# Mixture of softmaxes: giving each partition 32 adjacent rows instead of every 128th row

## The chip, the cores and the metric

The kernel runs on one core of a Trainium2 chip; the other cores are idle. The metric is the device time of one execution in microseconds (us). Before the change it is 783.3 us (783.3 to 783.43). "The profile" is a hardware trace of one execution; its span is some 2 us shorter than the timed run.

## The reference

```python
batch, seq, vocab, num_heads = 32, 128, 4096, 4
prior_probs = softmax(prior, axis=-1)       # prior  [32, 128, 4]
s = softmax(logits, axis=-1)                # logits [32, 128, 4, 4096], float32
mixture = sum(prior_probs[..., None] * s, axis=2)   # [32, 128, 4096]
```

Numpy's `exp`, maximum and sum are written here as `softmax`. There are 4096 rows (batch times seq). A row is four heads of 4096 floats, so 64 KB to read and 16 KB to write: 268.4 MB in and 67.1 MB out in all.

## The kernel before

A unit of work is one batch element: 128 rows, one to a partition. The load of a unit is one DMA of 8.39 MB (four DMAs of one head each for the first and the last three units), the store one DMA of 2.10 MB. ScalarE (ACT) does the exponentials with their sums, VectorE (DVE) scales and adds the heads, GpSimd (POOL) multiplies two columns for a coefficient. SyncE (SP) issues the loads, ACT most of the stores. Two load tiles alternate.

```python
def pieces(b):
    return 1 if b == 0 or b >= B - 3 else H
def load(b, eng=nc.sync):
    lt = lpool.tile([P, H, V], FP32, name="ltile")        # bufs=2
    n = pieces(b)
    for h in range(0, H, n):
        eng.dma_start(out=lt[:, h : h + n], in_=logits[b, :, h : h + n, :])
def store(b, lo=0, hi=V, eng=nc.sync):
    eng.dma_start(out=out[b, :, lo:hi], in_=accs[b][:, lo:hi])
# ... prior: softmax on [32, 128, 4], then four 32x32 transposes to pp [128, H, 32] ...
for b in range(B):
    # ... store(b - 1, eng=nc.scalar)
    for h in range(H):
        ex = nc.scalar.activation(et, lt[:, h], AF.Exp, accum_out=dsum[:, col])
        nc.vector.reciprocal(rden[:, col], dsum[:, col])
        # h == 0: acc = et * rden * pp;  else coeff = rden * pp; acc += et * coeff
    if b + 2 < B:
        load(b + 2)
```

The softmax here doesn't subtract the row's maximum and nothing guards it: scores larger than these inputs give would overflow.

## Time and profile before

| | before |
|---|---|
| time | 783.3 us |
| DVE busy, ACT busy | 68%, 60% of the span |
| DMA engines busy | 99.7% (two data queues) |
| moved | 335.67 MB at a mean 430 GB/s |

From the profile page of the kernel before, the DMA rows in 40 slices of the span, the packets, and the queues (packets, MB, share of 16 engines):

```profile
DMA  9999999999999999999999999999999999999998
GB/s 373 448 416 440 434 416 456 410 463 405 460 409 456 416 443 429 419 454 415 458 408 450 419 464 406 456 427 430 432 430 439 426 446 412 457 408 430 429 429 364
DMA packets 11143, 335.67 MB, mean 430 GB/s; under 512 B 1248, under 2 KB 1248, under 8 KB 1280
q1 hardware_dynamic: 7056, 276.83, 82.1%
q10 hardware_dynamic: 4080, 58.79, 17.6%
```

A 9 is 90% busy or more. The 16 DMA engines have no idle slice, so they bound the kernel. The table by stretches of the kernel before (start and end, length, busy time of DVE, ACT and POOL, granted clock, DMA share, GB/s) gives the rates:

```profile
0.00:20.00 20.00, 9.98 (x13) 10.60 (x7) 0.40 (x5) 1.00 0.93 377
200.00:400.00 200.00, 136.30 (x69) 120.65 (x66) 4.97 (x26) 1.00 1.00 433
400.00:600.00 200.00, 134.74 (x65) 116.94 (x64) 4.60 (x24) 1.00 1.00 434
760.00:782.00 22.00, 10.93 (x6) 3.71 (x2) 0.38 (x2) 1.00 0.84 359
```

From the waits (engine, line, what it waited for: us in total, times, longest) and from the instructions in order of time (start, length; the first exponential of unit 1, of unit 2 and of unit 28; units count from 0):

```profile
ACT ebuf L107 <- DMA ltile<-in_logits_dram: 241.0, 32, 18.0
45.37 3.62 ACT L107 ACTIVATE ebuf<-ltile 128x4096 f32<-128x4096 f32 x1 [18.04 <-DMA ltile<-in_logits_dram]
67.81 3.62 ACT L107 ACTIVATE ebuf<-ltile 128x4096 f32<-128x4096 f32 x1 [6.40 <-DMA ltile<-in_logits_dram]
696.72 3.62 ACT L107 ACTIVATE ebuf<-ltile 128x4096 f32<-128x4096 f32 x1 [8.14 <-DMA ltile<-in_logits_dram]
```

ACT waits for loads. From unit 2 to unit 28 there are 26 units, of (696.72 - 67.81) / 26 = 24.19 us each; a unit moves 10.49 MB.

### The profile page before, as it was taken

What the parts mean: (1) busy time and instruction counts of PE and PEld (TensorE: products, weight loads), DVE (VectorE), ACT (ScalarE), POOL (GpSimd) and SP (SyncE); (2) the same over time, 40 slices, a digit from 0 to 9 for tenths busy, and PEclk for the clock granted to TensorE, in tenths of its full rate; (3) what the DMA queues carried; (4) which work ended last, traced back from release to release, by engine and by line L of the source; (5) the groups of instructions that cost most, each with busy time, mean ns of one, the idle gap of its engine ahead of it and who ended that gap; (6) DMA issues with size and microseconds to landing.
All of it is one profiled execution on the core that took longest, in us unless ns stands there. A gap on an engine that the chain in (4) does not pass through costs nothing.

```text
span 781.3 us, 851 instructions
## 1 busy us (share of the span) xinstructions
DVE 527.9 (68%) x266; ACT 470.0 (60%) x258; POOL 18.6 (2%) x100
## 2 busy tenths in 40 slices
DVE  4647677666786666865668666677666776668994
ACT  5366556755567555575555765547655577558971
POOL 0000000000000000000000000000000000000000
DMA  9999999999999999999999999999999999999998
GB/s 373 448 416 440 434 416 456 410 463 405 460 409 456 416 443 429 419 454 415 458 408 450 419 464 406 456 427 430 432 430 439 426 446 412 457 408 430 429 429 364
DMA packets 11143, 335.67 MB, mean 430 GB/s; under 512 B 1248, under 2 KB 1248, under 8 KB 1280
## 3 DMA queue, kind: packets, MB, share of 16 engines
q1 hardware_dynamic: 7056, 276.83, 82.1%
q10 hardware_dynamic: 4080, 58.79, 17.6%
q14 instruction: 7, 0.06, 0.0%
HBM read 268.50 MB, written 67.11 MB: 430 GB/s over the span
## 4 chain that ended last, share of the span: by engine, by line
DMA 66%; ACT 14%; DVE 10%; issue 7%; SPq 0%; POOL 0%; DVEq 0%; POOLq 0%; ACTq 0%
DMA ltile<-in_logits_dram 66%; ACT ebuf L107 14%; DVE acc L128 9%; DVE ltile L128 1%; SPq L43 0%; POOL coeff L123 0%; DVE rden L116 0%; DVEq L166 0%; DVE ltile L118 0%; POOLq L166 0%; ACTq L107 0%
## 5 line engine op out<-in xcount | busy, mean ns | idle before, releaser
L107 ACT ACTIVATE ebuf<-ltile 128x4096 f32<-128x4096 f32 x120 | 433.0, 3609 | 284.5 <-DMA ltile<-in_logits_dram 241.0
L128 DVE SCALAR_TENSOR_TENSOR acc<-ebuf,coeff,acc 128x4096 f32<-128x4096 f32 x90 | 403.6, 4484 | 27.4 <-POOL coeff L123 27.4
L116 DVE RECIPROCAL rden<-dsum 128x1 f32<-128x1 f32 x128 | 20.4, 160 | 206.3 <-ACT ebuf L107 206.3
L118 DVE TENSOR_SCALAR acc<-ebuf,rden,pp 128x4096 f32<-128x4096 f32 x30 | 72.4, 2412 | 1.3 <-DVE rden L116 0.3
L123 POOL TENSOR_TENSOR coeff<-rden,pp 128x1 f32<-128x1 f32 x96 | 18.4, 191 | 748.1 <-DVE rden L116 748.1
L107 ACT ACTIVATE ltile<-ltile 128x4096 f32<-128x4096 f32 x8 | 28.9, 3608 | 4.3 <-DMA ltile<-in_logits_dram 4.3
L128 DVE SCALAR_TENSOR_TENSOR ltile<-ltile,coeff 128x4096 f32<-128x4096 f32 (+1 forms) x7 | 27.0, 3874 | 1.8 <-POOL coeff L123 1.8
L107 ACT ACTIVATION_READ_ACCUMULATOR ebuf<-ltile 128x1 f32 x120 | 22.4, 187 | 0.0
L118 DVE TENSOR_SCALAR ltile<-ltile,rden,pp 128x4096 f32<-128x4096 f32 x2 | 4.8, 2412 | 0.1
L58 DVE TENSOR_REDUCE pmax<-pr 32x128 f32<-32x512 f32 x1 | 0.7, 674 | 5.8 <-DMA pr<-in_prior_dram 5.8
L62 ACT ACTIVATE pe<-pc 32x512 f32<-32x512 f32 x1 | 0.6, 628 | 4.8 <-DVE pc L60 4.8
L62 ACT ACT_TABLE_LOAD x1 | 1.3, 1283 | 1.2 <-PEq L155 1.2
L107 ACT ACTIVATION_READ_ACCUMULATOR ltile<-ltile 128x1 f32 x8 | 1.5, 186 | 0.0
L75 DVE STREAM_TRANSPOSE pp<-pn 32x128 f32<-32x128 f32 x4 | 1.2, 302 | 0.1
L64 DVE TENSOR_REDUCE psum<-pe 32x128 f32<-32x512 f32 x1 | 0.7, 674 | 0.7 <-ACT pe L62 0.7
L69 DVE TENSOR_TENSOR pn<-pe,prec 32x512 f32<-32x512 f32 x1 | 1.0, 1042 | 0.0
L66 DVE RECIPROCAL prec<-psum 32x128 f32<-32x128 f32 x1 | 0.9, 941 | 0.0
L60 DVE TENSOR_TENSOR pc<-pr,pmax 32x512 f32<-32x512 f32 x1 | 0.7, 680 | 0.0
L155 POOL MEMSET const-float32-0.0<- 128x1 f32 x1 | 0.1, 99 | 0.2 <-issue 0.2
L155 POOL MEMSET const-bfloat16-1.0<- 128x1 bf16 x1 | 0.1, 102 | 0.0
L155 POOL MEMSET const-uint8-127<- 128x1 uint8 x1 | 0.1, 102 | 0.0
L155 POOL MEMSET const-float32-1.0<- 128x1 f32 x1 | 0.1, 99 | 0.0
## 6 DMA issues: line engine op xcount, KB each, us to landing
out_dram<-acc ACTq DMA_DIRECT2D x28, 2048.0 KB, 29.3
ltile<-in_logits_dram SPq DMA_DIRECT2D x16, 2048.0 KB, 20.5
out_dram<-acc SPq DMA_DIRECT2D x2, 2048.0 KB, 32.9
out_dram<-ltile SPq DMA_DIRECT2D x1, 2048.0 KB, 21.2
out_dram<-ltile SPq DMA_DIRECT2D x2, 1024.0 KB, 8.7
ltile<-in_logits_dram SPq DMA_DIRECT2D x28, 32.3
pr<-in_prior_dram ACTq DMA_DIRECT2D x1, 64.0 KB, 5.0
```

The source lines that it names most:

```text
L58: nc.vector.reduce_max(pmax, pr, axis=AX.X)
L60: nc.vector.tensor_sub(pc, pr, pmax.unsqueeze(2).to_broadcast([B, S, H]))
L62: nc.scalar.activation(pe, pc, AF.Exp)
L64: nc.vector.reduce_sum(psum, pe, axis=AX.X)
L66: nc.vector.reciprocal(prec, psum)
L69: nc.vector.tensor_mul(pn.rearrange("b h s -> b s h"), pe, prec.unsqueeze(2).to_broadcast([B, S, H]))
L75: nc.vector.transpose(pp[32 * t : 32 * (t + 1)], pn[:, :, 32 * t : 32 * (t + 1)])
L107: ex = nc.scalar.activation(et, lt[:, h], AF.Exp, accum_out=dsum[:, col])
L116: nc.vector.reciprocal(rden[:, col], dsum[:, col])
L118: nc.vector.tensor_scalar(out=acc, in0=et, scalar1=rden[:, col], scalar2=pp[:, h, b : b + 1], op0=ALU.mult, op1=ALU.mult,)
L123: nc.gpsimd.tensor_mul(coeff[:, col], rden[:, col], pp[:, h, b : b + 1])
L128: nc.vector.scalar_tensor_tensor(out=acc[:, cs], in0=et[:, cs], scalar=coeff[:, col], in1=acc[:, cs], op0=ALU.mult, op1=ALU.add,)
```

## The change

Each partition gets 32 adjacent rows of the whole input, and unit u is row u of every partition. Then `prior` arrives in the layout in which it is used, and its softmax needs no transposes and fewer tiles. Loads, stores and compute keep their number, shape and order. What else moves is where one DMA reads and writes: neighbouring partitions were 64 KB apart in `logits` and 16 KB in `out`, and are now 2 MB and 512 KB apart (the pitch). "Near" is used below for the old addresses, "wide" for the new ones.

```diff
+    U = B * S // P
+    lg = logits.rearrange("b s h v -> (b s) h v").rearrange("(p u) h v -> u p h v", u=U)
+    ov = out.rearrange("b s v -> (b s) v").rearrange("(p u) v -> u p v", u=U)
+    pv = prior.rearrange("b s h -> (b s) h").rearrange("(p u) h -> p u h", u=U)
...
-            eng.dma_start(out=lt[:, h : h + n], in_=logits[b, :, h : h + n, :])
+            eng.dma_start(out=lt[:, h : h + n], in_=lg[b, :, h : h + n, :])
...
-        eng.dma_start(out=out[b, :, lo:hi], in_=accs[b][:, lo:hi])
+        eng.dma_start(out=ov[b, :, lo:hi], in_=accs[b][:, lo:hi])
...
-    pr = cpool.tile([B, S, H], FP32, name="pr")        # and pc, pe, psum, prec, pn, 4 transposes
-    nc.scalar.dma_start(out=pr, in_=prior)
+    pr = cpool.tile([P, U, H], FP32, name="pr")        # sub, exp, sum, reciprocal in place
+    nc.scalar.dma_start(out=pr, in_=pv)
```

More of the change, by code (lines that the diff above doesn't have):

```diff
@@ L34, in pieces @@
     def pieces(b):
-        return 1 if b == 0 or b >= B - 3 else H
+        return 1 if b == 0 or b >= U - 3 else H
     ltiles = {}
@@ L48, in store @@
     def store(b, lo=0, hi=V, eng=nc.sync):
-        eng.dma_start(out=out[b, :, lo:hi], in_=accs[b][:, lo:hi])
+        eng.dma_start(out=ov[b, :, lo:hi], in_=accs[b][:, lo:hi])
     load(0, eng=nc.sync)
-    pr = cpool.tile([B, S, H], FP32, name="pr")
-    nc.scalar.dma_start(out=pr, in_=prior)
+    pr = cpool.tile([P, U, H], FP32, name="pr")
+    nc.scalar.dma_start(out=pr, in_=pv)
     load(1, eng=nc.sync)
-    pmax = cpool.tile([B, S], FP32, name="pmax")
+    pmax = cpool.tile([P, U], FP32, name="pmax")
     nc.vector.reduce_max(pmax, pr, axis=AX.X)
-    pc = cpool.tile([B, S, H], FP32, name="pc")
-    nc.vector.tensor_sub(pc, pr, pmax.unsqueeze(2).to_broadcast([B, S, H]))
-    pe = cpool.tile([B, S, H], FP32, name="pe")
-    nc.scalar.activation(pe, pc, AF.Exp)
-    psum = cpool.tile([B, S], FP32, name="psum")
-    nc.vector.reduce_sum(psum, pe, axis=AX.X)
-    prec = cpool.tile([B, S], FP32, name="prec")
-    nc.vector.reciprocal(prec, psum)
-    pn = cpool.tile([B, H, S], FP32, name="pn")
-    nc.vector.tensor_mul(
-        pn.rearrange("b h s -> b s h"), pe, prec.unsqueeze(2).to_broadcast([B, S, H])
-    )
-    pp = cpool.tile([P, H, B], FP32, name="pp")
-    for t in range(S // 32):
-        nc.vector.transpose(
-            pp[32 * t : 32 * (t + 1)], pn[:, :, 32 * t : 32 * (t + 1)]
-        )
+    nc.vector.tensor_sub(pr, pr, pmax.unsqueeze(2).to_broadcast([P, U, H]))
+    nc.scalar.activation(pr, pr, AF.Exp)
+    nc.vector.reduce_sum(pmax, pr, axis=AX.X)
+    nc.vector.reciprocal(pmax, pmax)
+    pp = cpool.tile([P, U, H], FP32, name="pp")
+    nc.vector.tensor_mul(pp, pr, pmax.unsqueeze(2).to_broadcast([P, U, H]))
     NCHUNK = 2
-    dsum = cpool.tile([P, B * H], FP32, name="dsum")
-    rden = cpool.tile([P, B * H], FP32, name="rden")
-    coeff = cpool.tile([P, B * H], FP32, name="coeff")
+    dsum = cpool.tile([P, U * H], FP32, name="dsum")
+    rden = cpool.tile([P, U * H], FP32, name="rden")
+    coeff = cpool.tile([P, U * H], FP32, name="coeff")
     ebuf = cpool.tile([P, 2, V], FP32, name="ebuf")
     exps = []
-    for b in range(B):
-        last = b == B - 1
-        inplace = b >= B - 2
+    for b in range(U):
+        last = b == U - 1
+        inplace = b >= U - 2
         lt = ltiles.pop(b)
@@ L99 @@
         acc = accs[b]
-        if 0 < b < B - 3:
+        if 0 < b < U - 3:
             store(b - 1, eng=nc.scalar)
@@ L118 @@
                 nc.vector.tensor_scalar(
-                    out=acc, in0=et, scalar1=rden[:, col], scalar2=pp[:, h, b : b + 1],
+                    out=acc, in0=et, scalar1=rden[:, col], scalar2=pp[:, b, h : h + 1],
                     op0=ALU.mult, op1=ALU.mult,
@@ L122 @@
                 continue
-            nc.gpsimd.tensor_mul(coeff[:, col], rden[:, col], pp[:, h, b : b + 1])
+            nc.gpsimd.tensor_mul(coeff[:, col], rden[:, col], pp[:, b, h : h + 1])
             n = NCHUNK if split else 1
@@ L133 @@
                     store(b, c * w, (c + 1) * w)
-        if b + 2 < B:
+        if b + 2 < U:
             load(b + 2)
-        if b == B - 3:
+        if b == U - 3:
             store(b - 1)
             store(b)
-        elif b == B - 2:
+        elif b == U - 2:
             store(b)
```

## The prediction

> **What bounds the kernel now.** The 16 DMA engines. The page's DMA row reads 9 (90% or more) in 39 of 40 slices and its two data queues take 82.1% and 17.6% of the engines' time, 99.7% together. They move 335.67 MB at a mean 430 GB/s; the table by stretches shows 433 to 434 GB/s from 100 to 600 us, and less only in the first 20 us (377) and the last 22 (359). DVE is busy 68%, ACT 60%. In the waits, ACT waited 241.0 us for loads of ltile. A unit (8.39 MB in, 2.10 MB out) costs 24.2 us of DMA (10.49 MB at 433 GB/s; the chain shows two units per 48.35 us), against 16.5 us of DVE (527.9/32). The Trainium skill, "DMA: Bandwidth & Descriptors", section "Bandwidth", gives a ceiling of 435 GB/s; the trace's 433 agrees. At 435 the bytes alone take 772 us: no layout gains 2%.
>
> **What the change does to instructions.** Loads, stores, exps and accumulations keep count, shape, engine and order, and each row of a load is still one run of 64 KB (16 KB for first and last units), of a store 16 KB. The prior chain shrinks: four transposes (1.25 us in all) go, and reductions, subtract, exp, reciprocal and multiply (0.67, 0.67, 0.68, 0.63, 0.94, 1.04 us at 32x512) run on 128x128, estimated at a quarter to a third. DVE's chain starts at 5.8 us when prior lands and ends at 11.9; after, about 8. But its first accumulation waits for the first exp (done at 12.6, itself waiting for a load), and DMA has two units queued ahead. Worth on the critical path: 0 to 0.3 us.
>
> **What it moves: HBM addresses.** Before, one load reads 8 MB that lie together, partitions 64 KB apart; a store writes 2 MB, 16 KB apart. After, partitions are 2 MB apart in logits and 512 KB apart in the output. The same skill page, section "Latency and other measured facts", entry "HBM row pitch at large powers of two", has 128 x 16 KiB copies between HBM tensors at 207 GB/s each way for 512 KiB, 164 for 2 MiB, 103 for 4 and 8 MiB and 214 unhindered. The trace before has only the small pitches, at full rate, so no run shows this yet. Estimate from the page and the trace: if loads keep 164/214 of 433 GB/s (332) and stores 207/214 (419), a unit takes 25.3 + 5.0 = 30.3 us, and the kernel about 970 + 9 of ends, 980. But that was HBM to HBM with two aliasing streams; here one side is SBUF, reads are 80% of traffic, rows are four times as long, and the engines may drift apart. A half-sized effect gives 27 us a unit, 880; none gives 782.
>
> **Prediction.** 880 us, range 780 to 985 (8 in 10). Chances: faster by 2% 0.01, within 2% 0.30, slower 0.69.
>
> **What would show it.** Right: DMA still over 95% busy, but steady GB/s down to 330 to 400 with the same bytes and packets; loads land later than 32.3 us; ACT's wait for ltile grows by nearly the whole difference (some 100 us); DVE and ACT busy times within 1% but for some 4 us of prior work; loads slow more than stores.  If the page's effect is absent, GB/s stays at 430 and the time between 780 and 784.
>
> **What would make it wrong.** Address interleaving over HBM channels that hashes high bits (no loss); or losses past the page's, when 2 MB reads and 512 KB writes collide with each other; or losses mostly from the stores.

## The result, and the profile after

The changed kernel takes 805.27 us median (803.03 to 807.88, four runs); before, 783.3 us. The ratio is 1.0281 (95% interval 1.0247 to 1.0316). All ratios here are the mean time of one kernel's fast runs over that of the kernel before, run beside it in the same session, so not quite the ratio of the medians. The result stays correct. The same lines of the profile page after:

```profile
DMA  8999999999999999999999999999999999999997
GB/s 349 419 407 407 436 413 435 427 426 432 422 428 436 420 435 431 424 426 433 420 432 420 433 420 432 419 437 421 425 418 434 432 424 418 425 414 391 414 398 325
DMA packets 11239, 335.67 MB, mean 419 GB/s; under 512 B 1248, under 2 KB 1376, under 8 KB 1376
q1 hardware_dynamic: 7056, 276.83, 82.1%
q10 hardware_dynamic: 4176, 58.79, 17.1%
```

The same bytes, the engines as busy, but 419 GB/s instead of 430. From the table by stretches of the kernel after:

```profile
0.00:20.00 20.00, 5.70 (x9) 9.27 (x7) 0.39 (x5) 1.00 0.85 350
200.00:400.00 200.00, 133.30 (x66) 120.70 (x69) 4.55 (x24) 1.00 1.00 427
400.00:600.00 200.00, 133.47 (x66) 119.99 (x65) 4.74 (x25) 1.00 1.00 426
780.00:802.00 22.00, 9.05 (x4) 3.71 (x2) 0.19 (x1) 1.00 0.75 320
```

And the wait of ACT and the same three instructions after (line 107 is now line 100):

```profile
ACT ebuf L100 <- DMA ltile<-in_logits_dram: 254.7, 31, 21.4
50.16 3.62 ACT L100 ACTIVATE ebuf<-ltile 128x4096 f32<-128x4096 f32 x1 [21.38 <-DMA ltile<-in_logits_dram]
72.79 3.62 ACT L100 ACTIVATE ebuf<-ltile 128x4096 f32<-128x4096 f32 x1 [6.59 <-DMA ltile<-in_logits_dram]
712.71 3.62 ACT L100 ACTIVATE ebuf<-ltile 128x4096 f32<-128x4096 f32 x1 [8.47 <-DMA ltile<-in_logits_dram]
```

This splits the 19.9 us by which the span grew. Unit 2 starts 72.79 - 67.81 = 5.0 us later; the 26 units from there to unit 28 take 639.92 instead of 628.91 us, 11.0 us more (24.61 us a unit, up 0.42); what is left after unit 28 takes 801.2 - 712.71 = 88.5 instead of 84.6 us, 3.9 more. So a small loss in every unit makes up over half, and the two ends the rest. At the start it is mostly the first load with 64 KB rows: unit 1 starts 50.16 - 45.37 = 4.8 us later, while the last exponential of unit 0, whose loads have 16 KB rows, starts only 1.4 us later (25.07 instead of 23.62 us). At the end the loads have 16 KB rows.

The trace also has one record for each row that a DMA engine moved, and these records tell which transfers slowed. From those records, of the load queue and the store queue (ns; here and below cut to whole ns):

```
                          before                    after
64 KB load rows   median 2418, mean 2421    median 2418, mean 2475, 90th percentile 2632
16 KB, queue q1   median  611, mean  616    median  611, mean  645, 90th percentile  728
16 KB store rows  median  611, mean  611    median  611, mean  611   (queue q10)
```

Loads are slower and stores are not. Two thirds of the 64 KB load rows still take 2418 ns, give or take 2; a quarter takes over 2468 ns (before, 1%). The queue q1 also holds the last few stores, so its 16 KB rows are nearly all loads. Summed over all records of q1 and divided by 16 engines, the excess is 16.2 of the 19.9 us: 12.0 in the 64 KB rows and some 4.2 in the 16 KB rows.

One thing differs in the first microseconds. The DMA issues (KB, us from issue to landing, which is when the last byte has arrived) and DVE's wait for `prior` (us in total, times, longest), before and then after:

```profile
pr<-in_prior_dram ACTq DMA_DIRECT2D x1, 64.0 KB, 5.0
DVE pmax L58 <- DMA pr<-in_prior_dram: 5.8, 1, 5.8
```

```profile
pr<-in_prior_dram ACTq DMA_DIRECT2D x1, 64.0 KB, 8.6
DVE pmax L64 <- DMA pr<-in_prior_dram: 9.4, 1, 9.4
```

`prior` now goes as 128 rows of 512 B instead of 32 of 2 KB: eight rows for each DMA engine instead of two. The Trainium skill, "DMA: Bandwidth & Descriptors", section "Queues, rings and completion order", says that an engine goes round between the queues that have work, a packet at a time. The trace agrees, with one row to a turn: rows of the two queues alternate on an engine, so its eight short rows wait behind some eight load rows of 0.61 us.

### The profile page after: what moved, and what is told of

Read it like the earlier page. It is cut to its first block, busy times and chain, and to the rows that moved or that the text cites. A ratio compares the mean times of both kernels' runs of the same rounds, so it can differ in the third digit from the quotient of the medians.

```text
span 801.2 us, 847 instructions
## 1 busy us (share of the span) xinstructions
DVE 524.6 (65%) x262; ACT 469.8 (59%) x258; POOL 18.4 (2%) x100
## 4 chain that ended last, share of the span: by engine, by line
DMA 66%; ACT 15%; DVE 10%; issue 7%; POOL 0%; DVEq 0%; SPq 0%; POOLq 0%; ACTq 0%
DMA ltile<-in_logits_dram 66%; ACT ebuf L100 15%; DVE acc L121 10%; ACT ltile L100 0%; POOL coeff L116 0%; DVE rden L109 0%; DVE ltile L121 0%; DVEq L159 0%; SPq L49 0%; POOLq L159 0%; ACTq L100 0%
```

## The experiments

The runs whose names begin with `bench` were executed once each, and they are read within one trace only. All others are variants of the kernel, timed four times each.

Theory A was that the 2 MB pitch of the reads slows them. Rivals were the 512 KB pitch of the stores (B), the wide spread of the addresses whatever the pitch (C) and the later `prior` (D).

### One part of the change at a time

`loads_wide`: the changed kernel with the stores as before. The rows of the output are then wrong.

```diff
-        eng.dma_start(out=ov[b, :, lo:hi], in_=accs[b][:, lo:hi])
+        eng.dma_start(out=out[b, :, lo:hi], in_=accs[b][:, lo:hi])
```

> The changed kernel with the output written as before (16 KB rows side by side), so only loads have the 2 MB pitch; wrong result on purpose. Theory A (the 2 MB read pitch alone slows the reads, as the packet times of the changed kernel say): 801 to 807 us, 64 KB load packets at a mean near 2475 ns. Rival B (the 512 KB write pitch, or its meeting the reads, costs the time): 783 to 786 us.

Measured: 806.5 us (800.89 to 809.09), ratio 1.0286. Load rows of 64 KB: mean 2484 ns.

`stores_wide`: the changed kernel with the loads as before. Its output is wrong, which doesn't matter for the time.

```diff
-            eng.dma_start(out=lt[:, h : h + n], in_=lg[b, :, h : h + n, :])
+            eng.dma_start(out=lt[:, h : h + n], in_=logits[b, :, h : h + n, :])
```

> The changed kernel with logits read as before (8 MB that lie together), so only stores have the 512 KB pitch; wrong result on purpose. Theory A: 783 to 785 us, load packets at 2418 ns. Rival B: 798 to 807 us.

Measured: 784.25 us (783.26 to 784.9), ratio 1.001 (0.9995 to 1.0025). Load rows: mean 2423 ns.

`prior_only`: both edits together, so only the prior part of the change is left. Its output is wrong, which doesn't matter for the time.

> The changed kernel with loads and stores as before, so only the handling of prior is new; wrong result on purpose. Theory A: 783 to 784 us though prior still lands near 9 us. Rival D (part of the loss is the later prior, 9.4 instead of 5.8 us): up to 787 us.

Measured: 783.1 us, ratio 0.9997. The new prior code costs and saves nothing that can be seen.

`pitch31`: each partition has 31 adjacent rows, and the 128 rows left over make the last unit. The result is right.

```diff
+    W = U - 1
+    N = P * W
+    lm = lf[0:N].rearrange("(p u) h v -> u p h v", u=W)      # lf: logits as (b s) h v
+    lg = [lm[u] for u in range(W)] + [lf[N:]]                # out and prior likewise
```

> Each partition has 31 adjacent rows (pitch 1.94 MB to read, 496 KB to write) and the last unit is 128 rows that lie together; right result. Theory A (a pitch of a large power of two is what hurts): 783 to 787 us. Rival C (reading 128 places spread over 256 MB hurts whatever the pitch): 798 to 807 us.

Measured: 783.33 us (783.03 to 783.95), ratio 1.0001. The tables by stretches of `loads_wide`, `stores_wide` and `pitch31`, in this order:

```profile
100.00:700.00 600.00, 396.09 (x196) 356.87 (x197) 13.98 (x73) 1.00 1.00 426
```

```profile
100.00:700.00 600.00, 404.58 (x197) 358.79 (x197) 14.17 (x74) 1.00 1.00 432
```

```profile
100.00:700.00 600.00, 404.93 (x197) 359.94 (x197) 14.17 (x74) 1.00 1.00 433
```

The last number is GB/s. Theory A holds alone: the wide loads bring the whole loss, and B and D fall. C falls too: 31 rows to a partition spread the reads almost as far as 32, and lose nothing. What costs is the pitch being a large power of two, or a multiple of one: a pitch such as 24 rows (1.5 MB) was not run, so these two are not told apart. What happens inside HBM was not measured. The 31-row kernel is as fast as the kernel before and no faster, and it needs no transposes either.

### Which pitch is large enough to cost

`pitch16` gives each partition 16 rows, in two groups of units; `pitch8`, `pitch4` and `pitch2` do the same with 8, 4 and 2 rows. All are right.

```diff
+    W = 16                                # 8, 4, 2
+    N = P * W
+    for g in range(U // W):
+        lm = lf[g * N : (g + 1) * N].rearrange("(p u) h v -> u p h v", u=W)
+        lg += [lm[u] for u in range(W)]   # out and prior likewise
```

> Each partition has 16 adjacent rows, in two groups of units: pitch 1 MB to read, 256 KB to write; right result. If the loss grows with the pitch as in the loads alone (1 MB lost 1 us in 8 units where 2 MB lost 8): 783 to 788 us. If any large power of two costs the same: 800 to 807 us.

> Each partition has 8 adjacent rows, in four groups: pitch 512 KB to read, 128 KB to write; right result. If the loss grows with the pitch: 783 to 785 us. If any large power of two costs the same: 800 to 807 us.

> Each partition has 4 adjacent rows, in eight groups: read pitch 256 KB, write 64 KB; right result. If the loss goes on down by halves of the pitch: 790 to 800 us; if it ends below 512 KB: 783 to 785 us.

> Each partition has 2 adjacent rows, in sixteen groups: read pitch 128 KB, write 32 KB; right result. Both theories: 783 to 787 us, close to the kernel before with its 64 KB.

| rows to a partition | read pitch | time, us | mean 64 KB load row, ns |
|---|---|---|---|
| 32 (the change) | 2 MB | 805.27 (803.03 to 807.88) | 2475 |
| 31 | 1.94 MB | 783.33 (783.03 to 783.95) | 2422 |
| 16 | 1 MB | 806.25 (804.34 to 809.73) | 2504 |
| 8 | 512 KB | 800.04 (785.95 to 804.7; three of four slow) | 2493 |
| 4 | 256 KB | 786.14 (785.48 to 787.03) | 2422 |
| 2 | 128 KB | 787.47 (787.22 to 787.52) | 2422 |
| 1 (before) | 64 KB | 783.3 (783.3 to 783.43) | 2421 |

My expectation for `pitch16` and `pitch8`, that the loss grows with the pitch, was wrong: 1 MB costs as much as 2 MB (ratio 1.0297). At 512 KB three of the four runs lost nearly as much and one lost 2.6 us. So 512 KB is unclear. At 256 KB and below no more 64 KB rows are slow than in the kernel before (1%).

The traces show two more things. These kernels load `prior` in 2, 4, 8 and 16 DMAs with ever shorter rows, and it lands at 14.9, 23.6, 17.3 and 18.1 us, where the changed kernel has 9.4. The 3 to 4 us that `pitch4` and `pitch2` cost lie before unit 2, which starts 2.5 and 3.9 us later than in the kernel before; the late `prior` is the likely cause, but no run shows it alone. And the traced run of `pitch8` (801.26 us) has slow load rows (27% over 2468 ns) in another order of work: DVE waits for stores, as the line of its page shows (busy us, mean ns, then the wait), where the kernel before has no such wait.

```profile
L122 DVE TENSOR_SCALAR acc<-ebuf,rden,pp 128x4096 f32<-128x4096 f32 x30 | 72.4, 2412 | 91.5 <-DMA out_dram<-acc 91.4
```

Its fast run (785.95 us) has no trace, so why that one escaped is open.

### Why the loss is small: loads alone, and copies

`bench_load` only loads, in phases of 8 units. Its output is wrong, which doesn't matter for the time.

```diff
+    def phase(views, n):
+        for v in views:
+            lt = lpool.tile([P, H, V], FP32, name="ltile")
+            for h in range(0, H, n):
+                nc.sync.dma_start(out=lt[:, h : h + n], in_=v[:, h : h + n, :])
+    phase(near[0:8], H)          # near, then 2 MB, 1 MB, 512 KB, 128 KB
+    phase(w2m[0:8], H)           # ... then 16 KB rows near and at 2 MB, then half loads
```

> Loads alone, no compute and no stores meanwhile, in phases of 8 units (67 MB): side by side; pitch 2 MB; 1 MB; 512 KB; 128 KB (all 64 KB rows); then 16 KB rows side by side and at 2 MB; then two half loads of 64 partitions at 2 MB and at 4 MB; wrong result on purpose. If a small loss in the kernel comes from the reads alone: the 2 MB phase at 415 to 427 GB/s against 430 to 434 side by side, 1 MB and below at most 1% short, 4 MB clearly worse than 2 MB (below 400). If reads only suffer beside writes: every phase within 1% of 432. If 16 KB rows are what made the figure cited in the prediction large: the 16 KB phase at 2 MB below 360 GB/s.

Here are the first loads, from the row records in order of time: us in which 128 rows were done, mean row, share of rows over 2468 ns.

```
near   1  19.35  2422   2%        2 MB   1  22.04  2707  68%
       2  19.39  2433  12%               2  21.49  2655  75%
       3  19.62  2452  23%               3  20.80  2555  48%
       4  19.56  2447  20%               4  19.56  2468  28%
       5  19.36  2422   3%               5  19.33  2463  23%
       6  19.32  2419   0%               6  19.32  2420   2%
       7  19.33  2420   0%               7  19.32  2427   6%
                                         8  19.45  2440  12%
```

The near load before the first of these starts from an empty queue and is left out. By this count the wide loads lose 2.7, 2.1 and 1.5 us; slow rows go on, fewer, to the fifth. By the landing of the last of a load's 16 parts the first five lose 2.7, 2.1, 1.4, 1.1 and 0.9 us, and then nothing. Meanwhile the 16 engines, whose parts of one load landed within 0.4 us of each other, come to land 4.1 us apart. I read this so (theory E): engines that go level, each at the same place in its share at the same time, get in each other's way, are pushed apart by it, and then run free. None of the three outcomes that I wrote down was this one.

Two parts of this run do not tell what they were made for. The 1 MB, 512 KB and 16 KB phases began with engines already 4 to 6 us apart and lost little, which is why I wrongly expected the loss to grow with the pitch. The half loads of 64 partitions, meant to compare a pitch of 2 MB with 4 MB, ran at 209 GB/s at both (length, POOL, clock, DMA share, GB/s):

```profile
1110.00:1400.00 290.00, 0.00 (x0) 1.00 1.00 209
1400.00:1740.00 340.00, 0.00 (x0) 1.00 1.00 209
```

The Trainium skill, "SBUF — State Buffer", section "Door 1: The DMA port swizzle", says that bandwidth depends on how many of the 16 ports the partitions reach, and partitions 0 to 63 reach half of them; 209 of 433 agrees. Whether 4 MB is worse is open.

`bench_copy` copies 128 x 16 KB from HBM to HBM, four times 32 copies. Its output is wrong, which doesn't matter for the time.

```diff
+    for b in range(B):           # near to near
+        nc.sync.dma_start(out=out[b], in_=logits[b, :, 0, :])
+    # then near <- wide, wide <- near, wide <- wide (2 MB), to another HBM tensor
```

> Copies from HBM to HBM of 128 x 16 KB in four phases of 32 copies: both sides near; read at 2 MB; write at 2 MB; both at 2 MB; wrong result on purpose. If the figure in the prediction holds here and belongs to copies with both sides in HBM: about 205 to 215 GB/s each way near, about 165 with both at 2 MB, and the phases with one wide side tell which side does it: reads (under 190 in the second phase) or writes (under 190 in the third). If it does not hold on this chip, all four are within 5% of each other.

From the table by stretches of `bench_copy`, one stretch inside each phase in this order (length, POOL, clock, DMA share, GB/s each way):

```profile
20.00:228.00 208.00, 0.00 (x0) 1.00 1.00 301
240.00:500.00 260.00, 0.00 (x0) 1.00 0.99 244
510.00:800.00 290.00, 0.00 (x0) 1.00 0.99 220
820.00:1180.00 360.00, 0.00 (x0) 1.00 0.99 177
```

Both sides cost, and neither alone fell under the 190 GB/s that I had set. A copy reads and writes HBM once for each byte, so HBM carried about 602 GB/s near, 488 with wide reads, 440 with wide writes and 354 with both. The 164 GB/s that the prediction cites for both at 2 MB is close to the 177 here; its 214 unhindered is not 301, but that was another layout than near here. The copies with wide reads still move 488 GB/s by this sum, more than the 433 of the kernel. As an estimate of what HBM could give the kernel this is rough: it is for a mix of one to one, and the kernel reads four bytes for each that it writes.

### Shorter rows

`rows16_wide` and `rows16_near` are the kernel after and before with one head to a load, so rows of 16 KB; `rows16_31` is the same edit on `pitch31`. All are right.

```diff
     def pieces(b):
-        return 1 if b == 0 or b >= U - 3 else H
+        return 1
```

> The changed kernel with every unit loaded as four loads of 16 KB rows, one head each, still 2 MB apart. If the short rows of the copies cited in the prediction made their loss larger: over 830 us. If a row's length does not matter: 803 to 815 us, as the changed kernel plus what the control adds.

> Control for the run before: the kernel before the change with every unit loaded as four loads of 16 KB rows. Both theories: 783 to 790 us, since each row is still 16 KB and a load 2 MB.

> The kernel with 31 rows to a partition with every unit loaded as four loads of 16 KB rows. If the larger loss of rows16_wide (829 against 790 us) comes from the power-of-two pitch as well: 788 to 792 us. If short rows far apart cost by themselves: over 800 us.

Measured: 829.44 us wide, 789.56 near, 789.44 with 31 rows. Against the kernel before of the same rounds the ratios are 1.0611, 1.0079 and 1.0078, so wide costs 1.0611 / 1.0079 = 1.053. The loss is about twice that with 64 KB rows. It is the pitch here as well, and short rows far apart cost nothing by themselves. Why short rows lose more was not found. `rows16_wide` fell just under the 830 us that I had set for "short rows matter", but it is well outside the 803 to 815 of the other outcome. This fits the end of the changed kernel, whose loads have 16 KB rows.

### Why it goes on in every unit

Loads alone recover after five units. The kernel never does. `bench_mix` was to show wide loads beside stores.

```diff
+    def beside(view, first):
+        for u in range(16):
+            lt = lpool.tile([P, H, V], FP32, name="ltile")
+            nc.sync.dma_start(out=lt, in_=view[u])
+            nc.scalar.dma_start(out=out[first + u], in_=st)
```

> No compute. Phases: 6 near loads each waiting for the one before (all engines start level each time); 6 wide loads (2 MB) the same; 16 near loads with a near store beside each, always queued; 16 wide loads with the same stores; wrong result on purpose. Theory E (streams that start level collide, are pushed apart and then run free): near 19.4 us a load plus the gap of the wait, wide 2 to 3 us more at every one of the six; beside stores the wide loads lose time in the first units only and then run at the near ones' 24.2 us. Rival F (writes in between keep the wide reads slow however long): the last wide loads still at 24.5 us or more.

It failed as an experiment: nothing held the stores back, so all 32 ran during the first 450 us, beside the wrong loads. `bench_mix2` makes each store wait for a load:

```diff
+    def store(lt):
+        st = spool.tile([P, V], FP32, name="st")
+        nc.vector.tensor_copy(st, lt[:, 0])
+        nc.scalar.dma_start(out=out[len(done)], in_=st)
```

> As bench_mix, with each store made to wait for a load, two stores ahead: 6 near loads and 6 wide loads (2 MB) each waiting for the one before, no stores; 12 near loads and then 20 wide loads, each with a near store beside it; wrong result on purpose. Theory E (engines that start level collide, are pushed apart and then run free): of the waiting loads every wide one takes 2 to 3 us more than a near one; beside stores the wide loads lose in the first units and end at the near ones' 24.2 us. Rival F (writes between keep wide reads slow however long): the last ten wide loads still at 24.5 us or more, with slow load packets to the end.

Its first 12 loads, meant as 6 near and then 6 wide, used different tiles and so ran alternately. Counted as before, all near ones but the first, which starts the queue, took 19.32 us. The wide ones took 23.55, 23.91, 21.01, 20.27, 21.07 and 19.51 us, while the engines went from 0.6 to 5.1 us apart. In the first of them all 128 rows were slow (mean 2932 ns): 19.32 / 23.55 = 0.82 of the speed, not far from the prediction's 164 / 214 = 0.77. Every row was slow only in this load, with the engines 0.6 us apart. But being apart did not free the later ones: with the engines 4.3 to 5.1 us apart, 38%, 49% and 21% of the rows of the last three wide loads were slow. So theory E holds in part.

Beside stores, from the table by stretches of `bench_mix2` (length, DVE, POOL, clock, DMA share, GB/s), near and then wide:

```profile
280.00:520.00 240.00, 20.65 (x9) 0.00 (x0) 1.00 1.00 434
540.00:1000.00 460.00, 45.11 (x20) 0.00 (x0) 1.00 1.00 427
```

These are the kernel's own rates before and after, with almost no compute. Near loads took 24.18 us each, the last nine full wide units 24.54 us on average. So theory E fell for loads beside stores: the engines were 6 to 10 us apart and the loss stayed. Rival F, that writes in between cost by themselves, was left.

The row records of the changed kernel showed where to look. On one engine a row of a load and a row of a store alternate; where an engine's eight rows of a store end, the record of its completion takes the turn, and two load rows follow each other. I call this the seam between two stores. I sorted the 64 KB load rows by the store row that went before on the same engine (records of an engine found by their ends meeting the next start; 110 to 690 us):

```
went before             rows   mean excess, ns   share over 2468 ns
completion of a store    379          65             31%
store row 1              377         134             60%
store row 2              376          94             47%
store row 3              374          32             21%
store row 4              375          15             10%
store row 8              262           0              0%
```

Rows 5 to 7 are left out; they have 6 to 13% slow rows. Just after the seam between two stores the loads are slow, and just before it they are not. The same sorting of `loads_wide` agrees (64% after row 1, 2% after row 8); in `pitch16` the row after the seam stands out as well (61%), but the last row is not free of it (19%). Theory G: at a seam an engine shifts by one store row, 0.6 us, against the others. It takes some 9 us until all engines have passed the seam, about the spread of their landings (6 to 9 us), and meanwhile streams that had kept out of each other's way meet again. `bench_seam` keeps the writes and takes away most seams, with stores four times as long:

```diff
+        to = out[first : first + n].rearrange("b s v -> (b s) v").rearrange("(p k) v -> p k v", k=n)
+        nc.scalar.dma_start(out=to, in_=st.unsqueeze(1).to_broadcast([P, n, V]))
+    # 12 wide loads beside stores with n = 1, then 20 beside stores with n = 4
```

> Wide loads (2 MB pitch) with stores always queued beside them, no compute: 12 loads beside stores of 128 rows (one seam between stores in each unit), then 20 beside stores of 512 rows (a seam in each fourth unit); wrong result on purpose. Theory G (the seams between stores shift the engines against each other and so renew the collisions): in the second part units without a seam at 24.2 to 24.3 us with mean load packets under 2430 ns, units with one at 24.4 to 24.9. Rival F (writes among wide reads cost by themselves): every unit of the second part at 24.4 to 24.9 us, as in the first.

From the row records (units of load counted from 0, with the start in units 0 to 2 left out; mean row, slow rows):

```
units  3 to 13, a seam in each          2433 to 2474 ns    9 to 27%
units 14 to 23 (a seam at 16/17, 20)    2418 to 2426 ns    0 to  2%
unit  24 (a seam)                       2495 ns           23%
units 25 to 32 (seams at 27/28, 31)     2418 to 2419 ns    0 to  2%
```

With writes beside all but the last load, the wide loads ran at full speed in 18 of the last 19 units, so F falls: writes as such do not slow them. Each of these loads has an end of its own too, so the ends of loads are not what renews the loss. The one slow unit had a seam. Seams at 16/17, 20, 27/28 and 31 did little harm, so by theory G a seam would renew the collisions only sometimes, one time in five in this part. The unit times that I had expected did not come out, for another reason: without seams nine store rows instead of eight go with a unit of loads, which takes 24.78 us at 433 GB/s. Theory G is supported, not closed: the longer stores also write other addresses in another order, and no run of the kernel itself was made without seams.

## Why the prediction was wrong

- Right: DMA bounds the kernel, the instructions matter little, no gain came, loads slow and stores do not, bytes stay, DMA stays busy. `prior` and its transposes are worth nothing.
- Right in direction: slower, from the 2 MB read pitch. `loads_wide` and `pitch31` show the cause by itself.
- Wrong in size. The step that failed is the term "if loads keep 164/214 of 433 GB/s", and with it "a half-sized effect gives 27 us a unit". A unit went from 24.19 to 24.61 us: 0.42 us more where the prediction had 2.8. Steady GB/s fell to 427, not to between 330 and 400, and ACT's wait for loads grew by 13.7 us, not by 100.
- What the runs showed in its place: the wide kernel keeps 427 / 434 = 0.98 of its rate, not 164/214 = 0.77. That share was one of copies with both sides in HBM; `bench_copy` finds a lasting loss in such copies (177 / 301 = 0.59), with both sides taking part. Among loads into SBUF the nearest to it was 0.82, in one load with the engines level; alone the loss was gone after five loads, and beside stores a quarter of the rows stayed slow. Of the doubts that the prediction named, the longer rows are shown: 16 KB rows double the loss, to 5.3%. So is that copies are another case: with 16 KB rows in both, copies with wide reads kept 244 / 301 = 0.81 of their rate and the kernel 1 / 1.053 = 0.95. Why loads into SBUF are hindered less is argued and not shown: that HBM is asked for less, or that the engines drift apart. Together these doubts should have weighed more than a half.
- A smaller miss: the prior chain was to end near 8 us. It ended at 11.4 us, because `prior` landed at 9.4 instead of 5.8 us. This cost nothing (`prior_only`: 783.1 us).
- The range, 780 to 985 us, held the 805 us; but it was so wide because it covered two outcomes, no effect and a large one, and had its middle where nothing was. That it held says little for the mechanism.

## What to carry to other kernels

When a layout changes, look at the distance in HBM between the partitions of one DMA, not only at the length of the rows: here 1 MB and 2 MB cost 3% (5% at 2 MB with 16 KB rows), 512 KB did in some runs, and a pitch of 31 rows instead of 32 cost nothing. A loss measured on copies is not to be multiplied into a kernel that does not copy; measure the kernel's own kind of transfer, with the row length that it has. In a benchmark with several phases, let each begin from the same state of the queues, or the order of the phases becomes the result.

## What the Trainium skill lacked or had wrong

- "DMA: Bandwidth & Descriptors", section "Latency and other measured facts", entry "HBM row pitch at large powers of two": copies here ran at 177 GB/s each way with both sides at 2 MB (164 there), and at 301 near, in another layout than its unhindered 214. It has no figure with one wide side: 244 for wide reads, 220 for wide writes.
- The same entry has copies only. Loads into SBUF lost up to 18% in their first units, nothing after five units alone, and 1.6% for good beside stores (427 against 434 GB/s).
- It has 512 KiB as nearly free (207 of 214); here, in loads, a read pitch of 512 KB cost 0.3 to 2.7% by the run, and 1 MB as much as 2 MB (ratio 1.0297). As a remedy it has padding or a contiguous layout; 31 rows to a partition instead of 32 also restored the full speed (ratio 1.0001), with no padding in HBM.
- No page has anything on slow rows at the seam between two DMAs of a queue: at 2 MB, 60% of the load rows after the first store row were slow, none just before the seam. That the seam is the cause is supported, not closed.
- No page has the cost of a small transfer whose many short rows alternate with another queue's long ones: 64 KB as 32 rows of 2 KB landed after 5.0 us, as 128 rows of 512 B after 8.6 us.
